# Hybrid mLSTM / neighbourhood / memory encoder layer on one Trainium2 core: the first loads and the last product rearranged

## Chip, core and metric

The kernel runs on one core of one Trainium2 (trn2) chip. The metric is the device time of one execution in microseconds (us). Engines: PE is TensorE (matmuls; PEld its weight loads), ACT is ScalarE, DVE is VectorE, POOL is GpSimd, SP is SyncE, which here issues every DMA.

## The reference, cut to what matters

One encoder layer over 2048 tokens of width 1024, all in float32. Three token mixers read one normalised input, are gated and merged, and go through `w_out` into the residual; a squared-ReLU MLP follows. At the two ends of the program, which the change touches, this is computed:

```
k, v = split(rmsnorm(mem, g_mem) @ w_mem_kv)     # 256 memory tokens: the first matmuls of the kernel
...
x = x + y @ w_out
u = rmsnorm(x, g_ffn) @ w_up
return x + square(relu(u)) @ w_down              # the last matmuls of the kernel, and the residual
```

## The kernel before, in words

**Arithmetic.** A float32 operand is split into a high part (`hi`, rounded to the PE's fp32r format by an ACT copy) and a low part (`lo = x - hi`, a DVE subtraction). `mm3` (L227 to L234) makes one product of three matmuls: hi*hi (L232), hi*lo (L233), lo*hi (L234). So the first of the three needs only the ACT copies, and the second needs the DVE's low part of the weights.

**Phases.** Phase 1 projects the input and runs the attention parts, phase 2 the mLSTM, phase 3 the merge, `w_out` and the MLP. The order of the PE's instructions is the program's own order (`manual_schedule`); on the other engines a scheduler orders the instructions when the program is built, by priority (program order, shifted by `cur_priority`) and readiness, and then each engine and each DMA queue works strictly in that order.

**Weights.** A weight unit is 128 x 1024 floats (512 KB). `fetch` (L156) takes the next unit of the plan: a DMA into a raw buffer (`wr`, a ring of WRAW = 3), then the ACT copy (L176) and the DVE subtraction (L177) into a split buffer (`ws`, a ring of WSP = 5). A raw buffer is free again when L177 has read it.

**The start** (`mem_setup`, L1085). SP issues `gmem`, then in turn two row blocks of `memT` (256 KB, L1094) and a unit of `w_mem_kv` (L172), four times. After the second pair come the first token tile `xt` and `gbc` (`prep_x`), whose square (L339), product (L341) and scaling (L342) stand among the splits on ACT and DVE. Each row block of `memT` is scaled and split into `hT` (ACT L1097, DVE L1098). Then PE runs the memory projection: for k = 0 to 7 two token tiles, three matmuls each, 48 matmuls of 128x512 in all; k = 0 and 1 use the first unit ("unit 0"), k = 2 and 3 unit 1, k = 4 and 5 unit 2, k = 6 and 7 unit 3. Jobs such as the transposes of the first token tile (L348) are slipped in between, and `block_a` follows.

**The end** (`mlp_down`, L1423). `w_down` is applied by a seven-product scheme (Strassen-Winograd) to a pair of token blocks. Each product runs over two slots of operands (`X`, split by L1461 and L1462), dq = 0 to 3, and within each dq over four token tiles t, each with a PSUM bank of its own: 4 x 4 x 3 = 48 matmuls. So all four banks are complete only in the last twelve matmuls. Then for each t DVE adds the bank to `acc` (L1488) and, where the output is final (`last`), forms `acc * r + x` with the residual `x` loaded from `x2` (L1495), and SP stores it (L101). The product that ends the kernel is number 6 (output 2).

Of the kernel before, what the change touches and what calls it, by code (L numbers as in the profile page):

```python
# [12 lines left out]
F32 = mybir.dt.float32  # L13
F32R = mybir.dt.float32r
BF16 = mybir.dt.bfloat16
AF = mybir.ActivationFunctionType
ALU = mybir.AluOpType
# [6 lines left out]
TB = 512  # L24
# [9 lines left out]
LATER_3 = 4  # L34
STORE = 'sync'
ORDER_0 = (2, 3, 0, 1)
WSP, WRAW, AHEAD = 5, 3, 5
NB = S // TB
SCRATCH = 1024
# [2 lines left out]
FF = 4096  # L42
# [38 lines left out]
class Body:  # L81
# [71 lines left out]
        up = [(u["up"][j][0], u["up"][j + 1][0], "sums") for j in range(0, FF // 128, 2)]  # L153
        return out + (u["proj"] + u["w_out"] + up) * (NB // 2)

    def fetch(self):  # L156

        nc = self.nc
        entry = self.wplan.pop(0)
        if len(entry) == 3:  # L160
            self.wready.append(self.fetch_sums(*entry[:2]))
            return
        i, nk = entry
        self.n += 1
        raw = self.p_w.tile([128, 1056], F32, name=f"wr_{self.n}", tag="wraw", bufs=WRAW)
        w = self.p_ws.tile([128, 2112], F32R, name=f"ws_{self.n}", tag="wsp", bufs=WSP)
        first = self.a["w_units"].shape[0]
        n = 1024 if i < first else 1056
        raw = raw[:, :n]

        w = w[:, :2 * n].rearrange("p (k l c) -> p l k c", k=nk, l=2)
        nc.sync.dma_start(raw, self.a["w_units"][i] if i < first else self.a["w_navm"][i - first])  # L172
        raw = raw.rearrange("p (k c) -> p k c", k=nk)
        prio = self.tc.cur_priority
        self.tc.cur_priority = prio + self.later
        nc.scalar.activation(w[:, 0], raw, AF.Copy)  # L176
        nc.vector.tensor_tensor(w[:, 1], raw, w[:, 0].bitcast(F32), ALU.subtract)  # L177
        self.tc.cur_priority -= self.later
        self.wready.append(w)
# [905 lines left out]
    def mem_setup(self):  # L1085
        nc, a, p_a = self.nc, self.a, self.p_a


        gm = p_a.tile([128, 8], F32, name="gmem")
        nc.sync.dma_start(gm, a["g_mem"])  # L1090
        mT = p_a.tile([128, 4 * 704], F32, name="memT", tag="nak", bufs=2)[:, :2 * D].rearrange("p (k t) -> p k t", k=8)
        later, self.later = self.later, 0
        for k in range(0, 8, 2):
            nc.sync.dma_start(mT[:, k:k + 2], a["memT"][k * 128:(k + 2) * 128].rearrange("(k p) t -> p k t", p=128))  # L1094
            for i in (k, k + 1):
                hi, lo, g = self.hT[:, 0, i, 0:256], self.hT[:, 1, i, 0:256], gm[:, i:i + 1]
                nc.scalar.activation(hi, mT[:, i], AF.Copy, scale=g)  # L1097
                nc.vector.scalar_tensor_tensor(lo, mT[:, i], g, hi.bitcast(F32), ALU.mult, ALU.subtract)  # L1098
            self.fetch()
            if k == 2:  # L1100
                self.prep_x(a["g_mix"])
        self.later = later
        w = self.take(4)
        self.prep_x()
        xs = p_a.tile([128, 4 * 704], F32, name="xstage", tag="nak", bufs=2)
        for i in range(2):
            self.prep_x(xt=xs[:, i * D:(i + 1) * D])
        gq = p_a.tile([128, 2], F32, name="gmqk_raw")
        nc.sync.dma_start(gq, a["g_mem_qk"])
        self.gmqk = p_a.tile([128, 2], F32, name="gmqk")  # L1110
        nc.vector.tensor_scalar(self.gmqk[:, 0:1], gq[:, 0:1], 0.125, None, ALU.mult)
        nc.vector.tensor_copy(self.gmqk[:, 1:2], gq[:, 1:2])
        self.mk = p_a.tile([128, 2, 2, 256], F32R, name="mk")
        self.mv = p_a.tile([128, 2, 256], F32, name="mv")
        ps = [self.ps("mx") for _ in range(2)]
        self.trans_x(MEM_T)
        for k in range(8):
            wk = w[k // 2]
            for t in range(2):
                self.mm3(ps[t], self.lhs_tok(self.hT, k, t), (wk[:, 0, k % 2], wk[:, 1, k % 2]), k == 0, k == 7)  # L1120
            self.tick()
        self.memz = []
        for t, p in enumerate(ps):
            z = self.t("zm", [128, 256], 4)
            nc.scalar.activation(z, p[:, 0:256], AF.Copy)
            nc.vector.tensor_copy(self.mv[:, t], p[:, 256:512])
            self.memz.append(z)
# [295 lines left out]
    def mlp_down(self, i, pair, then):  # L1423


        nc = self.nc
        S, T, B = (lambda n: ("s", n)), (lambda h, n: ("t", h, n)), (lambda h, n: ("b", h, n))

        products = ((("a", 0), B(0, 0), 0, False, 0), (("a", 1), B(0, 1), 1, False, 0), (S(1), T(1, 1), 0, True, 1),
                    (S(0), T(1, 0), 1, False, 3), (S(2), T(0, 0), 0, True, 3), (S(3), B(1, 1), 1, True, 1),  # L1430
                    (("a", 2), T(0, 1), 0, True, 2))
        acc = self.p_h.tile([128, 4, 4, 512], F32, name=f"acc{i}", tag="hT", bufs=1)
        todo = [(q + dq, p) for q in range(0, FF // 512, 2) for p in products for dq in range(2)]
        total, ready = len(todo), []
# [4 lines left out]
        ring = lambda n: [r for r in rings if r[0] <= n][-1]  # L1439

        def fetch():

            n = total - len(todo)
            q, (l, r, *_) = todo.pop(0)
            n0, _, places = ring(n)
            at = self.X[places[(n - n0) % len(places)]]
            raw = at[:, 1].bitcast(F32)
            raws = [raw[:, 0:2], raw[:, 2:4]]
            nc.sync.dma_start(raws[0], self.scr[l[0]][i][q][:, l[1]])
            if r[0] == "t":  # L1450
                nc.sync.dma_start(raws[1], self.scr["t"][q][:, r[1], r[2]])
            else:
                self.n += 1
                raws[1] = self.p_w.tile([128, 1056], F32, name=f"wr_{self.n}", tag="wraw", bufs=WRAW)[:, :1024].rearrange("p (u c) -> p u c", u=2)
                u = self.down[r[1] * FF // 256 + 2 * q][0]
                nc.sync.dma_start(raws[1], self.a["w_units"][u:u + 2, :, r[2] * 512:r[2] * 512 + 512].rearrange("u p c -> p u c"))
            prio = self.tc.cur_priority
            self.tc.cur_priority = prio + LATER_A
            for k, src in enumerate(raws):
                hi, lo = (at[:, h, 2 * k:2 * k + 2] for h in range(2))  # L1460
                nc.scalar.activation(hi, src, AF.Copy)  # L1461
                nc.vector.tensor_tensor(lo, src, hi.bitcast(F32), ALU.subtract)  # L1462
            self.tc.cur_priority -= LATER_A
            ready.append(at)
        sets = [[self.ps("mm") for _ in range(4)] for _ in range(2)]
        used, seen = 0, set()
        for q in range(0, FF // 256, 4):
            for _, _, s, more, out in products:
                for dq in range(4):
                    if dq % 2 == 0:  # L1470
                        while todo and len(ready) < ring(total - len(todo))[1]:
                            fetch()
                        if then and used in (32, 46):
                            self.load_mix(*then[used == 46])
                        used += 1
                        at = ready.pop(0)
                    d = dq % 2
                    for t, p in enumerate(sets[s]):
                        ts = slice(t * 128, t * 128 + 128)
                        self.mm3(p, (at[:, 0, d, ts], at[:, 1, d, ts]), (at[:, 0, 2 + d], at[:, 1, 2 + d]),  # L1480
                                 not more and dq == 0, dq == 3, more)
                last = q == FF // 256 - 4 and (out, s, more) in ((0, 1, False), (3, 0, True), (1, 1, True), (2, 0, True))
                for t, p in enumerate(sets[s]):
                    c = acc[:, out, t]
                    if out not in seen:
                        nc.scalar.activation(c, p, AF.Copy)
                    else:
                        nc.vector.tensor_tensor(c, c, p, ALU.add)  # L1488
                    if last:
                        j, half = out // 2, out % 2  # L1490
                        hs, r0 = slice(half * 512, half * 512 + 512), t * 128
                        x = self.ev()
                        nc.sync.dma_start(x, self.scr["x2"][pair[j]][r0:r0 + 128, hs])
                        n = 4 * pair[j] + t
                        nc.vector.scalar_tensor_tensor(x, c, self.r2[:, n:n + 1], x, ALU.mult, ALU.add)  # L1495
                        r0 += pair[j] * TB
                        self.store(self.a["out"][r0:r0 + 128, hs], x)
                seen.add(out)

            sets.reverse()  # L1500
# [75 lines left out]
```

## Time and profile before

| | us |
|---|---|
| three timed runs | 2989.27, 2983.28, 2989.30 (median 2989.27) |
| the profiled execution's own time | 2988.64 |
| its span (first to last instruction) | 2986.9 |
| PE busy | 2910.6 (97%) |
| DVE busy | 2070.4 (69%) |
| ACT busy | 1195.1 (40%) |
| mean granted PE clock | 0.995 of full speed |

The span is 1.74 us less than the execution's own time; the profile shows only the span. An engine's share is an average over three quite different phases. What an edit is worth has to be read at the place of the edit: what PE waits for there, what ends that wait, and where the next wait stands.

### The profile page before, as it was taken

What the parts mean: (1) busy time and instruction counts of PE and PEld (TensorE: products, weight loads), DVE (VectorE), ACT (ScalarE), POOL (GpSimd) and SP (SyncE); (2) the same over time, 40 slices, a digit from 0 to 9 for tenths busy, and PEclk for the clock granted to TensorE, in tenths of its full rate; (3) what the DMA queues carried; (4) which work ended last, traced back from release to release, by engine and by line L of the source; (5) the groups of instructions that cost most, each with busy time, mean ns of one, the idle gap of its engine ahead of it and who ended that gap; (6) DMA issues with size and microseconds to landing.
All of it is one profiled execution on the core that took longest, in us unless ns stands there. A gap on an engine that the chain in (4) does not pass through costs nothing.

```text
span 2986.9 us, 41900 instructions
## 1 busy us (share of the span) xinstructions
PE 2910.6 (97%) x15028; PEld 2374.8 (80%) x15028; DVE 2070.4 (69%) x3557; ACT 1195.1 (40%) x2198; POOL 237.1 (8%) x389
## 2 busy tenths in 40 slices
PE   8999999999999899999999999999999999999999
PEld 6778788878877677778888888888878888888887
DVE  6676775567654765674769888666676888885666
ACT  6454654344543333342233333543312433344331
POOL 3020210011000322330000000000000000000000
PEclk9999999999999999999999999999999999999999
DMA  8776777867799667789535444766874444466655
GB/s 276 225 253 202 231 227 240 266 217 217 240 283 307 195 199 234 240 276 315 183 110 169 155 152 155 275 191 224 268 235 128 137 155 151 154 226 225 195 182 165
DMA packets 341712, 632.97 MB, mean 212 GB/s; under 512 B 29344, under 2 KB 151008, under 8 KB 341504
## 3 DMA queue, kind: packets, MB, share of 16 engines
q1 hardware_dynamic: 341504, 630.30, 65.4%
q8 instruction: 118, 1.93, 0.3%
q14 instruction: 90, 0.74, 0.1%
HBM read 453.63 MB, written 176.55 MB: 211 GB/s over the span
## 4 chain that ended last, share of the span: by engine, by line
PE 55%; DVE 2%; DMA 2%; issue 1%; ACT 0%; POOL 0%; SPq 0%; DVEq 0%; ACTq 0%; POOLq 0%
PE mm L232 18%; PE mm L234 18%; PE mm L233 18%; PE mm L1339 0%; DVE h L900 0%; DMA og<-s_o 0%; DMA wr<-in_w_units_dram 0%; DMA hf<-s_hf 0%; DVE ev L1495 0%; ACT hf L896 0%; POOL rs L325 0%; DVE acc L1488 0%; DVE ws L177 0%; DVE h L888 0%; DMA X<-s_a 0%
## 5 line engine op out<-in xcount | busy, mean ns | idle before, releaser
L232 PE MATMUL mm<-X,ws 128*128 128x512 f32 x1152 | 448.5, 389 | 0.0
L234 PE MATMUL mm<-X,ws 128*128 128x512 f32 x1152 | 448.2, 389 | 0.0
L233 PE MATMUL mm<-X,ws 128*128 128x512 f32 x1152 | 448.1, 389 | 0.0
L232 PE MATMUL mm<-hT,ws 128*128 128x512 f32 x896 | 375.6, 419 | 12.1 <-ACT cz L654 5.5
L177 DVE TENSOR_TENSOR ws<-wr,ws 128x1024 fp32r<-128x1024 f32 (+1 forms) x212 | 263.0, 1246 | 142.8 <-ACT ws L176 137.7
L234 PE MATMUL mm<-hT,ws 128*128 128x512 f32 x896 | 353.6, 395 | 0.0
L233 PE MATMUL mm<-hT,ws 128*128 128x512 f32 x896 | 353.4, 394 | 0.0
L233 PE MATMUL mm<-X 128*128 128x512 f32 x896 | 348.8, 389 | 2.5 <-DVE X L1462 2.5
L234 PE MATMUL mm<-X 128*128 128x512 f32 x896 | 348.7, 389 | 0.5 <-DVE X L1462 0.5
L232 PE MATMUL mm<-X 128*128 128x512 f32 x896 | 348.7, 389 | 0.4 <-ACT X L1461 0.4
L1461 ACT ACTIVATE X<-X 128x1024 fp32r<-128x1024 f32 x176 | 187.0, 1063 | 319.4 <-DMA X<-s_t 124.5
L1462 DVE TENSOR_TENSOR X<-X 128x1024 fp32r<-128x1024 f32 x176 | 214.3, 1224 | 132.8 <-ACT X L1461 132.0
L176 ACT ACTIVATE ws<-wr 128x1024 fp32r<-128x1024 f32 (+1 forms) x212 | 223.5, 1059 | 164.7 <-PE mm L234 91.8
L232 PE MATMUL mm<-ws,hT 128*128 128x512 f32 (+2 forms) x704 | 260.9, 371 | 9.3 <-ACT cz L654 5.1
L234 PEld LDWEIGHTS mm<-X,ws 128*128 128x128 f32 x1152 | 216.2, 188 | 45.1
L233 PEld LDWEIGHTS mm<-X,ws 128*128 128x128 f32 x1152 | 216.2, 188 | 44.9
L232 PEld LDWEIGHTS mm<-X,ws 128*128 128x128 f32 x1152 | 216.2, 188 | 44.5
L234 PE MATMUL mm<-ws,hT 128*128 128x512 f32 (+2 forms) x704 | 249.8, 355 | 1.1 <-DVE hT L434 1.1
L233 PE MATMUL mm<-ws,hT 128*128 128x512 f32 (+2 forms) x704 | 249.0, 354 | 0.3 <-DVE ws L177 0.3
L202 ACT ACTIVATE ws<-wr 128x512 fp32r<-128x512 f32 x224 | 135.3, 630 | 219.9 <-PE mm L234 139.3
L232 PEld LDWEIGHTS mm<-hT,ws 128*128 128x128 f32 x896 | 170.2, 190 | 54.1 <-issue 9.8
L234 PEld LDWEIGHTS mm<-hT,ws 128*128 128x128 f32 x896 | 169.6, 189 | 39.0
(266 smaller groups left out, 4855.3 us busy)
## 6 DMA issues: line engine op xcount, KB each, us to landing
wr<-in_w_units_dram SPq DMA_DIRECT2D x308, 512.0 KB
s_s<-u SPq DMA_DIRECT2D x32, 1024.0 KB
X<-s_s SPq DMA_DIRECT2D x64, 512.0 KB
X<-s_t SPq DMA_DIRECT2D x64, 512.0 KB
s_g<-ev SPq DMA_DIRECT2D x96, 256.0 KB
ev<-s_g SPq DMA_DIRECT2D x96, 256.0 KB
s_a<-u SPq DMA_DIRECT2D x96, 256.0 KB
X<-s_a SPq DMA_DIRECT2D x48, 512.0 KB
```

Of the source, the lines that this page charges most:

```text
L176: nc.scalar.activation(w[:, 0], raw, AF.Copy)
L177: nc.vector.tensor_tensor(w[:, 1], raw, w[:, 0].bitcast(F32), ALU.subtract)
L202: nc.scalar.activation(hi, src, AF.Copy)
L232: mm(out, lhs[0], rhs[0], start=first, stop=False)
L233: mm(out, lhs[0], rhs[1], start=False, stop=False)
L234: mm(out, lhs[1], rhs[0], start=False, stop=last)
L1461: nc.scalar.activation(hi, src, AF.Copy)
L1462: nc.vector.tensor_tensor(lo, src, hi.bitcast(F32), ALU.subtract)
```

## The change

It has two parts, at the two ends of the program.

*At the start*, 11 matmuls of the 128x128 matrix `ones` with itself (plain f32) go to PE ahead of everything, into a PSUM tile that nobody reads. The first `memT` load is cut into its two row blocks, and the first weight unit is loaded and split in two halves of 128 x 512 (k = 0 and k = 1), each with its own ACT copy and DVE subtraction. SP's order becomes: memT block 0, unit 0 half 0, unit 0 half 1, memT block 1, then as before.

*At the end*, the last product of all runs token tile by token tile: t outside, dq inside, so that a bank is complete after each twelve matmuls. Ahead of it, both its slots are taken, the four residual tiles are loaded, and `acc * r` is added to each of them. After each tile's twelve matmuls one DVE instruction forms `psum * r + x`, and the tile is stored. The other products keep their order.

```diff
+WARM = 11
...
-    def fetch(self):
+    def fetch(self, halves=False):
...
-        nc.sync.dma_start(raw, self.a["w_units"][i] if i < first else self.a["w_navm"][i - first])
+        src = self.a["w_units"][i] if i < first else self.a["w_navm"][i - first]
+        if halves:
+            src, r = src.rearrange("p (k c) -> p k c", k=nk), raw.rearrange("p (k c) -> p k c", k=nk)
+            for k in range(nk):
+                nc.sync.dma_start(r[:, k], src[:, k])
+                nc.scalar.activation(w[:, 0, k], r[:, k], AF.Copy)
+                nc.vector.tensor_tensor(w[:, 1, k], r[:, k], w[:, 0, k].bitcast(F32), ALU.subtract)
+            self.wready.append(w)
+            return
+        nc.sync.dma_start(raw, src)
...
+        p = self.ps("mx")
+        for i in range(WARM):
+            nc.tensor.matmul(p[:, 0:128], self.ones, self.ones, start=True, stop=True)
...
         for k in range(0, 8, 2):
-            nc.sync.dma_start(mT[:, k:k + 2], a["memT"][k * 128:(k + 2) * 128].rearrange("(k p) t -> p k t", p=128))
+            load = lambda i, n: nc.sync.dma_start(mT[:, i:i + n], a["memT"][i * 128:(i + n) * 128].rearrange("(k p) t -> p k t", p=128))
+            if k == 0:
+                load(0, 1)
+                self.fetch(True)
+                load(1, 1)
+            else:
+                load(k, 2)
...
-            self.fetch()
+            if k:
+                self.fetch()
...
+        def part(p, at, t, dq, more):
+            d, ts = dq % 2, slice(t * 128, t * 128 + 128)
+            self.mm3(p, (at[:, 0, d, ts], at[:, 1, d, ts]), (at[:, 0, 2 + d], at[:, 1, 2 + d]),
+                     not more and dq == 0, dq == 3, more)
...
+        def finish(out, t, x, src):
+
+            r0, hs, r = place(out, t)
+            nc.vector.scalar_tensor_tensor(x, src, r, x, ALU.mult, ALU.add)
+            self.store(self.a["out"][r0:r0 + 128, hs], x)
...
+                if q == FF // 256 - 4 and n == 6:
+
+                    ats, xs = [slot(), slot()], [x2(out, t) for t in range(4)]
+                    for t in range(4):
+                        nc.vector.scalar_tensor_tensor(xs[t], acc[:, out, t], place(out, t)[2], xs[t], ALU.mult, ALU.add)
+                    for t, p in enumerate(sets[s]):
+                        for dq in range(4):
+                            part(p, ats[dq // 2], t, dq, more)
+                        finish(out, t, xs[t], p)
+                    break
```

`slot` is the old code that takes the next slot, `x2` the old load of the residual tile, `place` the old row and column arithmetic, each as a function.

## Rows read from the trace of the kernel before

**Rows 1.** Page, busy time and share of the span of the engines.

```profile
PE 2910.6 (97%) x15028; PEld 2374.8 (80%) x15028; DVE 2070.4 (69%) x3557; ACT 1195.1 (40%) x2198; POOL 237.1 (8%) x389
```

**Rows 2.** Timeline, end of the span: start, duration, engine, line, what, idle before.

```profile
2967.74 1.37 DVE L1488 TENSOR_TENSOR acc<-acc,mm 128x512 f32<-128x512 f32 x2 [5.67 <-PE mm L234]
...
2971.54 1.41 DVE L1495 SCALAR_TENSOR_TENSOR ev<-acc,r,ev 128x512 f32<-128x512 f32 x2
...
2978.62 1.37 DVE L1488 TENSOR_TENSOR acc<-acc,mm 128x512 f32<-128x512 f32 x2 [5.67 <-PE mm L234]
...
2980.23 0.39 PE L234 MATMUL mm<-X 128*128 128x512 f32 x1
...
2982.42 1.41 DVE L1495 SCALAR_TENSOR_TENSOR ev<-acc,r,ev 128x512 f32<-128x512 f32 x2
2983.20 0.99 SPq L101 DMA_DIRECT2D out_dram<-ev  x2
```

**Rows 3.** Timeline, SP's queue near the end: the last residual loads.

```profile
2962.52 3.35 SPq L1493 DMA_DIRECT2D ev<-s_x  x3
```

**Rows 4.** One line's instructions: a scalar_tensor_tensor that reads PSUM (ns min/median/max).

```profile
L1286 DVE SCALAR_TENSOR_TENSOR ev<-ev,mm x96: 679/686/690, 1402.7 to 2276.1; 128x512 f32<-128x512 f32 x96
```

**Rows 5.** Timeline, PE's first products.

```profile
7.50 0.80 PE L232 MATMUL mx<-ws,hT 128*128 128x512 f32 x1 [7.50 <-ACT ws L176]
8.76 0.80 PE L233 MATMUL mx<-ws,hT 128*128 128x512 f32 x1 [0.46 <-DVE ws L177]
...
12.34 0.63 PE L232 MATMUL mx<-ws,hT 128*128 128x512 f32 x1
...
12.76 0.46 PE L233 MATMUL mx<-ws,hT 128*128 128x512 f32 x1
...
15.83 0.39 PE L234 MATMUL mx<-ws,hT 128*128 128x512 f32 x1
...
16.05 0.39 PE L232 MATMUL mx<-ws,hT 128*128 128x512 f32 x1
...
16.73 0.50 PE L233 MATMUL mx<-ws,hT 128*128 128x512 f32 x1 [0.29 <-DVE ws L177]
```

**Rows 6.** Timeline, ACT and DVE at the start, up to unit 2's low part.

```profile
1.07 0.17 DVE L283 MEMSET ones<- 128x128 f32 x1
...
10.06 1.23 DVE L177 TENSOR_TENSOR ws<-wr,ws 128x1024 fp32r<-128x1024 f32 x1 [0.57 <-ACT ws L176]
...
12.25 0.91 ACT L1097 ACTIVATE hT<-memT,gmem 128x256 fp32r<-128x256 f32 x2 [0.89 <-DMA memT<-in_memT_dram]
...
13.32 1.15 ACT L342 ACTIVATE xt<-xt,rs 128x1024 f32<-128x1024 f32 x1 [0.16 <-POOL rs L325]
...
14.38 1.05 ACT L176 ACTIVATE ws<-wr 128x1024 fp32r<-128x1024 f32 x1
...
15.45 1.22 DVE L177 TENSOR_TENSOR ws<-wr,ws 128x1024 fp32r<-128x1024 f32 x1 [1.78 <-ACT ws L176]
```

**Rows 7.** Timeline, SP's first issues.

```profile
1.23 0.42 SPq L1094 DMA_DIRECT2D memT<-in_memT_dram  x1
1.70 0.46 SPq L172 DMA_DIRECT2D wr<-in_w_units_dram  x1
```

**Rows 8.** Busy time by stretch: PE, PEld, DVE, ACT, POOL, granted clock, DMA share, GB/s.

```profile
8.00:13.00 5.00, 4.54 (x11) 3.38 (x11) 4.09 (x6) 3.21 (x6) 1.47 (x2) 1.00 1.02 392
...
60.00:90.00 30.00, 26.25 (x147) 22.17 (x146) 24.39 (x49) 11.08 (x23) 7.30 (x4) 0.94 0.87 270
```

**Rows 9.** Timeline, a pair of f32 matmuls of 128 columns.

```profile
1054.46 0.38 PE L838 MATMUL mx<-ident,qk 128*128 128x128 f32 x2
```

**Rows 10.** Timeline, PE's next wait after the memory projection, and ACT ahead of it.

```profile
23.27 1.06 ACT L176 ACTIVATE ws<-wr 128x1024 fp32r<-128x1024 f32 x1 [0.51 <-DMA wr<-in_w_units_dram]
...
31.15 0.50 PE L234 MATMUL mm<-ws,hT 128*128 128x512 f32 x1 [1.10 <-DVE hT L434]
```

**Rows 11.** Timeline, PE after a longer wait, in the stretch from 60 to 90.

```profile
80.07 0.39 PE L232 MATMUL mm<-ws,hT 128*128 128x272 f32 x1 [2.37 <-ACT cz L654]
```

More of the change, by code (lines that the diff above doesn't have):

```diff
@@ L1466, in mlp_down, with slot @@
         used, seen = 0, set()
-        for q in range(0, FF // 256, 4):
-            for _, _, s, more, out in products:
-                for dq in range(4):
[L1470 to L1477, printed above, removed]
+        def slot():
+            nonlocal used
+            while todo and len(ready) < ring(total - len(todo))[1]:
+                fetch()
+            if then and used in (32, 46):
+                self.load_mix(*then[used == 46])
+            used += 1
+            return ready.pop(0)
@@ new lines, in part, with place, x2 @@
+        def part(p, at, t, dq, more):
+            d, ts = dq % 2, slice(t * 128, t * 128 + 128)
+            self.mm3(p, (at[:, 0, d, ts], at[:, 1, d, ts]), (at[:, 0, 2 + d], at[:, 1, 2 + d]),
+                     not more and dq == 0, dq == 3, more)
+        def place(out, t):
+            j, half, n = out // 2, out % 2, 4 * pair[out // 2] + t
+            return n * 128, slice(half * 512, half * 512 + 512), self.r2[:, n:n + 1]
+        def x2(out, t):
+            x = self.ev()
+            r0, hs, _ = place(out, t)
+            b = r0 // TB
+            nc.sync.dma_start(x, self.scr["x2"][b][r0 - b * TB:r0 - b * TB + 128, hs])
+            return x
@@ new lines, in finish @@
+        def finish(out, t, x, src):
+            r0, hs, r = place(out, t)
+            nc.vector.scalar_tensor_tensor(x, src, r, x, ALU.mult, ALU.add)
+            self.store(self.a["out"][r0:r0 + 128, hs], x)
+        for q in range(0, FF // 256, 4):
+            for n, (_, _, s, more, out) in enumerate(products):
+                if q == FF // 256 - 4 and n == 6:
[7 more added lines that the diff above has]
+                    break
+                for dq in range(4):
+                    at = at if dq % 2 else slot()
@@ L1478, in mlp_down @@
                     for t, p in enumerate(sets[s]):
[L1479 to L1482, printed above, removed]
+                        part(p, at, t, dq, more)
+                last = q == FF // 256 - 4 and (out, s, more) in ((0, 1, False), (3, 0, True), (1, 1, True))
@@ L1489, in mlp_down @@
                     if last:
[L1490 to L1497, printed above, removed]
+                        finish(out, t, x2(out, t), c)
                 seen.add(out)
```

## The prediction
> **What bounds the kernel now.** I read the busy shares first: PE is busy for 97% of the span [rows 1], so nothing but PE time, or time in which PE cannot run, is to be won. The 76 us of its idle time lie in many places; the change touches two, the first 17 us and the last 6. About 0.2% (6 us) is what a measurement of this kernel can tell from no change, so the question is whether these two places together hold that much.
>
> *The end.* The last matmul of the program starts at 2980.23 and ends at 2980.62. DVE then is in the middle of eight instructions that it began at 2978.62, when the first of the four banks was complete; the last residual is formed at 2983.83, and the last store is issued behind it [rows 2]. From there to the end of the span (2986.9) are 3.07 us of store and closing. So 3.21 us of DVE work lie bare behind PE.
>
> *The start.* PE's first product waits until 7.50, its second until 8.76, both for unit 0's split; between 8.76 and 12.76 nine products start in 4.00 us, 0.44 each, where from 15.83 to 16.05 the distance is 0.22 to 0.23 [rows 5]. That is the low and the high level of the clock (1.2 and 2.4 GHz); the granted-clock column reads 1.00 in that stretch [rows 8], so I go by the distance. Then comes the row that decides: at 16.73 PE waits again, for the low part of unit 2 [rows 5]. That part is formed by DVE from 15.45 to 16.67, from ACT's copy at 14.38, which stands in ACT's queue behind a scaling at 13.32 and two `memT` splits at 12.25; and those waited 0.89 us for their load [rows 6]. In that stretch the DMA share is 1.02 at 392 GB/s [rows 8]: the loads come as fast as they can. So PE's progress before 16.73 does not matter; the load stream sets that point.
>
> **The change part by part.**
>
> *Last product by token tile.* The 48 matmuls stay 48 with the same shapes; PE ends at 2980.62 as before. Bank 3 is complete only there, but banks 0 to 2 are complete 12, 24 and 36 matmuls earlier (12 x 0.227 = 2.72 us apart). Removed behind PE: what is left of four additions and four residual steps. Added behind PE: one scalar_tensor_tensor that reads PSUM, 0.69 us by the nearest row of that kind [rows 4]. DVE is done at 2980.66 + 0.69 = 2981.35 in place of 2983.83: **-2.48 us**. The four additions made beforehand (4 x 0.70 = 2.8 us, half a pair's 1.41) have the time from 2972.95, when DVE ends the product before [rows 2], to 2980.66, and only 2.1 us of earlier tiles' final steps beside them: they cost nothing, and without that cover 2.8 us. Their residual loads are the same four, issued by 2965.87 [rows 3], 4 us before the product starts; both operand slots were split long before. What is late next is the store itself: its 3.07 us stay. Bounds: one more DVE instruction before the last one leaves 1.7; if the last store, now without a neighbour issued 0.66 us ahead of it, also lands that much sooner, 3.1.
>
> *Halves of the first unit.* Half a copy, half a subtraction and half a load (256 KB at 392 GB/s) are 0.53 + 0.61 + 0.65 us less before the second product, and the second `memT` block (128 KB, 0.33 us) goes behind: about 2.1 us earlier, an estimate from those rows [rows 6, 8]. *Products of ones.* If the clock is high by then, nine products cost 2.0 us in place of 4.0 [rows 5]: 2.0 more. PE would be 4.1 us ahead. But then it has unit 1 to wait for (its low part ends at 11.29 [rows 6]), needs 11 x 0.227 us from there, is done at 13.8, and stands until unit 2's low part at 16.67. **All of it goes into that wait: 0 us.** Even with the clock low throughout the old kernel came to that point with no more than 0.7 us to spare, so neither edit can show behind it.
>
> Does unit 2 move? SP gets two more issues, 0.47 us each [rows 7]: everything behind is issued 0.94 us later, but with the DMA engines full (share 1.02) an issue is not what is late; without that cover, +0.94. The bytes and their order are the same. ACT and DVE get one instruction more each for unit 0, hidden in their waits before 12.25. If the scheduler put unit 2's copy ahead of the scaling at 13.32, unit 2 would come 1.06 us sooner. So the start lies between -1.06 and +0.94; I take 0, as the queues' order follows a program order that the change leaves alone there.
>
> **Sum**: 2988.64 - 2.48 + 0 = **2986.2 us** for the profiled execution, which lies 0.63 below the median of the three runs (2989.27).
>
> **The rivals.**
>
> *The start comes through.* If unit 2 is not the wall that I read (the scheduler orders the first 30 us anew, so that loads and splits keep up), the whole 4.1 us could reach the end: 2982.1. For it: the first 12 us of PE are plainly slow. Against: two further waits of the same kind, the one at 16.73 and one of 1.10 us at 31.15, the latter behind a DVE queue that starts from a load landing at 23.27 [rows 10].
>
> *A new gap brings the low clock back.* PE now stands from 13.8 to 16.7 with one product between. In the stretch 60 to 90 a wait of 2.37 us [rows 11] goes with a granted clock of 0.94 [rows 8]: 6% of 30 us, 1.8 us of PE time. Here that would strike the products after 16.7; the 1.10 us that PE waits at 31.15 [rows 10] take up most, 0.7 is left: 2986.9, and 2988.0 if none is taken up. The Trainium skill's page "TensorE: Matmul & The Clock Gate", section "Why this matters for your kernels", recommends a warm-up by matmuls and says that gaps between bursts bring the low clock back. By its first half the products of ones would be worth the 2.0 us of clock; the trace agrees on the slow first products, but the wait at 16.73 stands behind them. Its second half is this rival, and the stretch with 0.94 agrees with it.
>
> *The products of ones hold PE up* (slower). PE works in order, so the first real product waits for all 11. An f32 matmul appears as a pair of instructions: 0.38 us a pair at the high clock [rows 9], so at most 0.38 a piece at the low one. `ones` is written by 1.24 [rows 6]; 22 x 0.38 from 1.3 ends at 9.7, and the 24 products of units 0 and 1 (5.4 us at the high clock) still end at 15.1, before the wall. Above 0.44 us a piece they pass it. The other end is PE's first lone product, 0.80 [rows 5]: 17.6 + 5.4 us end at 24.3, 7.9 late, 6.8 after the slack at 31.15: 2993.0. It makes the kernel slower than before from 0.60 a piece on. Against: the pair has just this shape, and the 0.80 is a 512-column product.
>
> *The end does not shrink.* If the additions beforehand stand behind a late residual load, or the scheduler puts them last, the 2.48 is gone: 2988.6.
>
> **How the numbers follow.** Forecast 0.67; start comes through 0.14; low clock 0.09; end does not shrink 0.06; ones hold PE up 0.04. The forecast's own range is 2985.5 to 2987.9 by its bounds on the end and to about one us more either way by those on the start. The executions before lie between 2983.28 and 2989.30, which alone is 0.2%. Low end: the start comes through (2982.1), less 0.6 for the upper bound of the end: 2981.5. High end: the end does not shrink, with the 0.94 of the issues: 2989.6. Faster by over 0.2% means below 2983.3: the start coming through, and a little of the spread: 0.17. Slower by over 0.2%: above 2995.2: 0.04, the ones and some reordering. The rest, 0.79, is within 0.2%.
>
> **What would show it.** Right: PE's second product near 6.7 and at the high clock, but a longer wait at 16.7 for unit 2's low part, and from there the old times; at the end one DVE instruction of 0.7 us behind PE's last matmul, and the span 2.5 us shorter. Wrong: unit 2's low part ready well before 16.67, or PE's wait at 31.15 gone and everything after it earlier; slow products after 16.7; real products that wait for ones; or additions of `acc * r` behind PE's last matmul.

## The result, and the profile after

| | kernel before | changed kernel |
|---|---|---|
| median of 8 runs each | 2989.28 us | 2995.51 us |
| lowest and highest | 2980.35 and 2993.09 | 2991.38 and 2998.77 |
| the profiled execution's own time | 2988.64 | 2995.25 |
| its span | 2986.9 | 2993.5 |

The changed kernel is slower: ratio 1.0029, 95% interval 1.0019 to 1.0039, which is 8.7 us (the two medians are 6.2 us apart). The forecast was 2986.2 with a range from 2981.5 to 2989.6; the measured time lies above the range, on the side that had a chance of 0.04. The engines' busy times hardly differ [rows 1]; PE is busy for longer than before, with 22 instructions more:

```profile
PE 2919.1 (98%) x15050; PEld 2383.3 (80%) x15050; DVE 2070.2 (69%) x3558; ACT 1195.7 (40%) x2199; POOL 236.6 (8%) x389
```

To see where the time went I laid the two traces side by side and took, for each product, its start after less its start before. At 12.3 us PE is 4.0 us ahead; at 16.7 it is 1.2 behind, at 31 2.3 behind. Over the middle of the program this goes up and down by some microseconds: it is -0.8 at 2137 and +0.6 at 2175.6. Within one product it then jumps to +9.2, and it is still +9.0 at the last matmul. So three places have to be read: the two that the prediction looked at, and one at 2176 us that it did not.

**The end** came out as predicted. Timeline of the changed kernel, DVE, then PE's last matmul (start, duration, engine, line, what, idle before):

```profile
2982.71 0.74 DVE L1526 SCALAR_TENSOR_TENSOR ev<-acc,r,ev 128x512 f32<-128x512 f32 x1
...
2986.93 0.75 DVE L1518 SCALAR_TENSOR_TENSOR ev<-mm,r,ev 128x512 f32<-128x512 f32 x1 [1.97 <-PE mm L244]
2989.65 0.75 DVE L1518 SCALAR_TENSOR_TENSOR ev<-mm,r,ev 128x512 f32<-128x512 f32 x1 [1.97 <-PE mm L244]
...
2989.23 0.39 PE L244 MATMUL mm<-X 128*128 128x512 f32 x1
```

The fourth early addition (L1526) is over long before the last bank is complete. One DVE instruction stands behind PE's last matmul; DVE is done 0.78 us after PE (2990.40 - 2989.62), where it was 3.21 us [rows 2], and 3.1 us of store and closing follow as before.

**The start.** Timeline of the changed kernel, PE up to 34 us:

```profile
1.28 5.06 PE L1104 MATMUL mx<-ones 128*128 128x128 f32 x22 [1.28 <-DVE halo L402]
5.99 0.61 PE L242 MATMUL mx<-ws,hT 128*128 128x512 f32 x1
...
8.75 0.39 PE L244 MATMUL mx<-ws,hT 128*128 128x512 f32 x1
11.23 0.50 PE L242 MATMUL mx<-ws,hT 128*128 128x512 f32 x1 [2.10 <-ACT ws L186]
12.49 0.50 PE L243 MATMUL mx<-ws,hT 128*128 128x512 f32 x1 [0.76 <-DVE ws L187]
...
13.44 0.63 PE L243 MATMUL mx<-ws,hT 128*128 128x512 f32 x1
13.87 0.63 PE L244 MATMUL mx<-ws,hT 128*128 128x512 f32 x1
...
17.89 0.50 PE L243 MATMUL mx<-ws,hT 128*128 128x512 f32 x1 [0.76 <-DVE ws L187]
...
33.48 0.72 PE L244 MATMUL mm<-ws,hT 128*128 128x512 f32 x1 [2.26 <-DVE hT L444]
```

The first twelve real products now run from 5.99 to 8.75, 0.25 us each: the high clock almost from the start, and 4 us earlier. But PE then waits for unit 1, the clock falls (0.43 between the starts at 13.44 and 13.87; the granted clock of 13 to 17 us is 0.57), and the wait for unit 2's low part ends at 17.89, where it was 16.73 [rows 5]. DVE, then ACT, of the same stretch:

```profile
11.22 1.23 DVE L187 TENSOR_TENSOR ws<-wr,ws 128x1024 fp32r<-128x1024 f32 x1 [1.45 <-ACT ws L186]
...
16.62 1.23 DVE L187 TENSOR_TENSOR ws<-wr,ws 128x1024 fp32r<-128x1024 f32 x1 [1.75 <-ACT ws L186]
...
13.45 0.91 ACT L1117 ACTIVATE hT<-memT,gmem 128x256 fp32r<-128x256 f32 x2 [0.86 <-DMA memT<-in_memT_dram]
```

Units 1 and 2 are split 1.16 and 1.17 us later than before, and the `memT` load ahead of unit 2 comes 1.20 later [rows 6]. The DMA engines are as busy as before, but move less. Busy time from 4 to 8 us (PE, PEld, DVE, ACT, POOL, granted clock, DMA share, GB/s), the changed kernel and then the kernel before:

```profile
4.00:8.00 4.00, 4.00 (x19) 3.69 (x19) 2.26 (x4) 1.76 (x4) 0.00 (x0) 1.00 0.94 297
```

```profile
4.00:8.00 4.00, 0.50 (x1) 0.29 (x1) 1.40 (x3) 2.52 (x5) 0.00 (x0) 1.00 0.92 332
```

**The first call of `mlp_down`.** This is where the jump is. Timeline of the changed kernel, PE, around the seventh product of the first pair of token blocks (the first row is its first matmul, the last row the first matmul behind it):

```profile
2176.14 0.50 PE L242 MATMUL mm<-X 128*128 128x512 f32 x1 [0.15 <-ACT X L1482]
...
2178.64 0.50 PE L242 MATMUL mm<-X 128*128 128x512 f32 x1
2186.77 0.79 PE L243 MATMUL mm<-X 128*128 128x512 f32 x1 [7.62 <-DVE X L1483]
...
2190.34 0.61 PE L242 MATMUL mm<-X 128*128 128x512 f32 x1
2190.77 0.42 PE L243 MATMUL mm<-X 128*128 128x512 f32 x1
...
2198.09 0.39 PE L242 MATMUL mm<-X,ws 128*128 128x512 f32 x1
```

The same product of the kernel before:

```profile
2175.55 0.50 PE L232 MATMUL mm<-X 128*128 128x512 f32 x1 [0.35 <-ACT X L1461]
...
2181.94 0.39 PE L232 MATMUL mm<-X 128*128 128x512 f32 x1
2183.53 0.50 PE L233 MATMUL mm<-X 128*128 128x512 f32 x1 [1.20 <-DVE X L1462]
...
2188.87 0.39 PE L232 MATMUL mm<-X,ws 128*128 128x512 f32 x1
```

From its first matmul to the next product's: 13.32 us before, 21.95 after. The branch of the change asks for `q` and `n`, not for the call, and `mlp_down` is called twice. So the section on the change is wrong where it says that the last product of all has the new order and the others keep theirs: the seventh product of the first call has it too. In the second call all operands are there. In the first one the ring of operand slots is two deep for its last slots (`rings`, the entry with 2), since `load_mix` for the merge takes the other buffers, and a slot is split just when it is needed. In the old order PE needs the second slot after 24 matmuls; token tile by token tile it needs it after 6. And its splits stand in DVE's queue behind the early additions. The loads are not what is late: ACT's copy for this slot is done at 2178.59, while DVE works without a break until 2186.71. DVE of the changed kernel, then of the kernel before:

```profile
2181.05 0.74 DVE L1526 SCALAR_TENSOR_TENSOR ev<-acc,r,ev 128x512 f32<-128x512 f32 x1
2181.71 0.74 DVE L1518 SCALAR_TENSOR_TENSOR ev<-acc,r,ev 128x512 f32<-128x512 f32 x1
2182.37 2.07 DVE L1526 SCALAR_TENSOR_TENSOR ev<-acc,r,ev 128x512 f32<-128x512 f32 x3
2184.36 2.35 DVE L1483 TENSOR_TENSOR X<-X 128x1024 fp32r<-128x1024 f32 x2
```

```profile
2180.45 1.23 DVE L1462 TENSOR_TENSOR X<-X 128x1024 fp32r<-128x1024 f32 x1
...
2182.25 1.22 DVE L1462 TENSOR_TENSOR X<-X 128x1024 fp32r<-128x1024 f32 x1
```

The longer wait is 6.4 us of the 8.6. The rest is the clock: behind the gap the products start 0.43 us apart until 2190.77, at the low level, and 0.23 after. Busy time by stretch (columns as above), the changed kernel and then the kernel before:

```profile
8.00:13.00 5.00, 2.15 (x8) 1.23 (x8) 2.31 (x4) 3.12 (x5) 0.25 (x2) 1.00 1.01 371
...
2160.00:2190.00 30.00, 21.65 (x86) 16.63 (x85) 21.57 (x28) 6.07 (x6) 0.00 (x0) 0.84 0.80 278
```

```profile
2160.00:2190.00 30.00, 27.92 (x121) 22.14 (x120) 22.07 (x29) 6.25 (x6) 0.00 (x0) 1.00 0.83 281
```

PE's waits over the whole span, that for the low part of `X` alone (us in total, times, longest), after and before:

```profile
PE mm L243 <- DVE X L1483: 10.2, 2, 7.6
```

```profile
PE mm L233 <- DVE X L1462: 2.5, 2, 1.3
```

### The profile page after: what moved, and what is told of

Same layout as the page of the kernel before. It is cut to its first block, busy times and chain, and to the rows that moved or that the text cites. A ratio compares the mean times of both kernels' runs of the same rounds, so it can differ in the third digit from the quotient of the medians.

```text
span 2993.5 us, 41949 instructions
## 1 busy us (share of the span) xinstructions
PE 2919.1 (98%) x15050; PEld 2383.3 (80%) x15050; DVE 2070.2 (69%) x3558; ACT 1195.7 (40%) x2199; POOL 236.6 (8%) x389
## 4 chain that ended last, share of the span: by engine, by line
PE 58%; DVE 2%; DMA 1%; ACT 1%; issue 1%; POOL 0%; SPq 0%; DVEq 0%; ACTq 0%; POOLq 0%
PE mm L242 19%; PE mm L243 19%; PE mm L244 19%; PE pn L872 1%; PE mm L1360 0%; DMA hf<-s_hf 0%; DMA wr<-in_w_units_dram 0%; PE pn L875 0%; DVE h L910 0%; PE mx L881 0%; ACT hf L906 0%; POOL rs L335 0%; DVE ev L1518 0%; DMA X<-s_a 0%; DVE acc L1542 0%
## 5 line engine op out<-in xcount | busy, mean ns | idle before, releaser
L242 PE MATMUL mm<-hT,ws 128*128 128x512 f32 x896 | 376.4, 420 | 10.5 <-ACT cz L664 5.5
L242 PEld LDWEIGHTS mm<-hT,ws 128*128 128x128 f32 x896 | 170.5, 190 | 52.7 <-issue 8.3
L243 PEld LDWEIGHTS mm<-X 128*128 128x128 f32 x896 | 169.1, 189 | 46.1 <-DVE X L1483 10.9
```

The costliest lines, as they stand in the source:

```text
L242: mm(out, lhs[0], rhs[0], start=first, stop=False)
L243: mm(out, lhs[0], rhs[1], start=False, stop=False)
```

## The experiments

A ratio is to the kernel before, run beside the experiment on the same chip, with its 95% interval (the medians of the kernel before: 2986.45 us beside experiments 1 to 4, 2985.22 beside 5 to 8, 2986.51 beside 9 to 12, 2985.52 beside 13 to 15). The edits are given against the changed kernel or against an earlier experiment.

**1. The whole start, the end in the last call only.**

```diff
-                if q == FF // 256 - 4 and n == 6:
+                if q == FF // 256 - 4 and n == 6 and not then:
...
-                last = q == FF // 256 - 4 and (out, s, more) in ((0, 1, False), (3, 0, True), (1, 1, True))
+                last = q == FF // 256 - 4 and (out, s, more) in ((0, 1, False), (3, 0, True), (1, 1, True), (2, 0, True))
```

> The changed kernel with one condition more: the last product goes token tile by token tile only in the second call of mlp_down (the one that ends the kernel); the first call keeps the old order. Theory A: the loss sits in the first call, where the product's second operand slot is needed after 12 matmuls and not after 24, and waits 7.62 us in the changed kernel (9.0 us with the clock that falls). Then the loss is gone and the gain at the end stays: 2989.3 - 2.4 = 2986.9, between 2984 and 2989, and no wait of several us near 2180. Rival B: the later loads of the start (shift +3.9 us at 33 us) carry through, and the wait near 2187 is only where that lands: then it stays at 2992 or more. Rival C: the scheduler's new order in phases 1 and 2 is the cause: also above 2990.

Median 2990.48, ratio 1.0012 [1.0001, 1.0023]. The wait in the first call is 1.21 us again and the product takes 13.32. So the loss in the first call is gone, as theory A has it; the time is above theory A's range all the same, and what the whole start has to do with that is taken up in 9 to 15. (The expectation says that the slot is needed after 12 matmuls; by the edit and the trace it is after 6.)

**2. The start alone**: the kernel before with the halves, the new order of loads and the 11 products of ones.

> The kernel before with the start of the change alone (products of ones, halves). Theory A: no loss and no gain that lasts, 2989.3 with 2 us either way; unit 2's low part comes about 1.2 us later than in the kernel before, as in the changed kernel, and later waits take that up. Rival B: 2993 to 2996. If the start is worth its 4 us after all: 2985.

Median 2988.55, ratio 1.0004 [0.9995, 1.0012]: theory A, within the runs' spread.

**3. The end in both calls, with the old start**: the kernel before with the new `mlp_down`.

> The kernel before with the last product's new order in both calls and the old start. Theory A: a wait of 6 to 8 us in the first call's last product, the low clock behind it, and 2.4 us less at the end: 2989.3 + 9 - 2.4 = 2996, between 2993 and 2998. Rival B: the wait is that of the kernel before (1.2 us), and the time 2987.

Median 2992.08, ratio 1.0018 [1.0007, 1.0030]. The time lies 0.9 us below theory A's range; PE's timeline has the long wait that it foresaw, without anything of the start:

```profile
2182.49 0.79 PE L233 MATMUL mm<-X 128*128 128x512 f32 x1 [7.51 <-DVE X L1462]
```

**4. The end in the last call only, with the old start**: experiment 3 with the edit of experiment 1.

> The kernel before with the new order in the last call alone, old start. All theories: the end is 2.4 us shorter (one DVE instruction of 0.75 us behind PE's last matmul), all else as in the kernel before: 2986.9. Nothing is moved ahead of the last call, so the order of the queues before it is the old one; if the time differs by more than 1 us from this, the runs' own spread is that large.

Median 2984.16, ratio 0.9992 [0.9982, 1.0003]. Timeline of the end, DVE and PE:

```profile
2980.67 0.75 DVE L1497 SCALAR_TENSOR_TENSOR ev<-mm,r,ev 128x512 f32<-128x512 f32 x1 [1.97 <-PE mm L234]
...
2980.24 0.39 PE L234 MATMUL mm<-X 128*128 128x512 f32 x1
```

This execution's last matmul happens to start at the very time of the kernel before (2980.23 [rows 2]); its span is 2984.4 in place of 2986.9. From the start of the last matmul to the end of the span it is 4.16 us in place of 6.67, and 4.16 again in experiment 11, where that matmul starts at 2973.64. So the end alone is worth 2.5 us, as predicted, and experiments 3 and 4, which differ in the first call alone, are 0.26% (7.9 us) apart.

**5. Only the order of the matmuls in the first call** (experiment 4, and there the tile order without early additions).

```diff
+                if q == FF // 256 - 4 and n == 6:
+
+                    ats = [slot(), slot()]
+                    for t, p in enumerate(sets[s]):
+                        for dq in range(4):
+                            part(p, ats[dq // 2], t, dq, more)
+                        c = acc[:, out, t]
+                        nc.vector.tensor_tensor(c, c, p, ALU.add)
+                        finish(out, t, x2(out, t), c)
+                    break
```

> The kernel with the new end in the last call alone and the old start (2984.2 before), plus this in the first call: its last product goes token tile by token tile, but the residual is not added beforehand; each tile is added to acc and finished as in the kernel before. So DVE's queue ahead of the second slot's splits is the old one, and only the need for that slot comes earlier. Theory A1, both halves share the loss: the slot's first low part is done at about 2183.5 as in the kernel before, PE asks for it at 2178.9; the wait is about 4.5 us, of which 2.7 are lost (12 products that could be done meanwhile are not), and up to 2 us of low clock: 2987 to 2989. Theory A2, the early additions alone make the loss: 2984. Theory A3, the order of the tiles alone makes it: 2992, wait 7 us.

**6. Only the early additions in the first call** (experiment 4, and there the old order with the additions ahead).

```diff
+                if q == FF // 256 - 4 and n == 6:
+
+                    ats, xs = [slot(), slot()], [x2(out, t) for t in range(4)]
+                    for t in range(4):
+                        nc.vector.scalar_tensor_tensor(xs[t], acc[:, out, t], place(out, t)[2], xs[t], ALU.mult, ALU.add)
+                    for dq in range(4):
+                        for t, p in enumerate(sets[s]):
+                            part(p, ats[dq // 2], t, dq, more)
+                    for t, p in enumerate(sets[s]):
+                        finish(out, t, xs[t], p)
+                    break
```

> The same base; in the first call the four residual tiles are loaded and added beforehand, as in the changed kernel, but the product runs in the old order (second slot after 24 products). Theory A1: the four additions of 0.75 us stand ahead of the second slot's two low parts in DVE's queue, which end at about 2186.7 in place of 2183.5; PE asks at 2182.2, waits 4.4 us in place of 1.2: 2987 to 2989.5. Theory A2: 2992. Theory A3: 2984.

Medians 2989.04 (ratio 1.0015 [1.0004, 1.0026]) and 2986.43 (1.0003 [0.9993, 1.0013]). Against experiment 4, their base (0.9992, on another chip), that is +0.23% and +0.11%. Runs alone would not part experiment 6 from the kernel before; the traces do. PE of experiment 5, then of experiment 6 with its DVE:

```profile
2172.55 0.50 PE L232 MATMUL mm<-X 128*128 128x512 f32 x1 [0.39 <-ACT X L1461]
...
2180.53 0.79 PE L233 MATMUL mm<-X 128*128 128x512 f32 x1 [4.95 <-DVE X L1462]
...
2192.05 0.39 PE L232 MATMUL mm<-X,ws 128*128 128x512 f32 x1
```

```profile
2167.58 0.41 PE L232 MATMUL mm<-X 128*128 128x512 f32 x1
...
2178.11 0.50 PE L233 MATMUL mm<-X 128*128 128x512 f32 x1 [3.81 <-DVE X L1462]
...
2180.09 0.63 PE L234 MATMUL mm<-X 128*128 128x512 f32 x1
...
2185.10 0.39 PE L232 MATMUL mm<-X,ws 128*128 128x512 f32 x1
...
2173.72 2.07 DVE L1515 SCALAR_TENSOR_TENSOR ev<-acc,r,ev 128x512 f32<-128x512 f32 x3
2175.70 2.35 DVE L1462 TENSOR_TENSOR X<-X 128x1024 fp32r<-128x1024 f32 x2
```

The table takes the seventh product of the first call from its first matmul to the first behind it, as above.

| first call | PE's wait for the slot's low part | the product takes |
|---|---|---|
| as before (kernel before) | 1.20 us | 13.32 us |
| early additions alone (6) | 3.81 | 17.52 |
| tile order alone (5) | 4.95 | 19.50 |
| both (3; changed kernel; the same again, 9) | 7.51; 7.62; 7.60 | 22.24; 21.95; 22.89 |

Each half costs by itself, the order 6.2 us and the additions 4.2; together it is 8.6 to 9.6. This is theory A1. The two halves can be told apart in DVE's queue: the low part that PE waits for is done 7.9 us after the product's first matmul in the kernel before and in experiment 5, 10.6 and 10.5 in the changed kernel and experiment 6. So the additions make the slot later, and the order makes PE ask sooner. The added waits sum up (3.75 + 2.61 = 6.36, against 6.31 to 6.42 with both); the low clock behind the wait comes in each case, but with both only once: in experiment 6 some eight products start 0.43 us apart instead of 0.23, 1.6 us.

**7 and 8. The parts of the start, with the end in the last call only**: experiment 4 with the 11 products of ones alone, and experiment 4 with the halves and the new order of loads alone.

> New end in the last call alone, plus the eleven products of ones at the start; loads whole as in the kernel before. If my reading of the start holds: the first products of PE run at the high clock, unit 2's low part stands where it stood (begins 15.3 to 15.6), the time is that without the ones, 2984.2, within 1.5 us. If the ones hold PE or bring a low clock in a later gap: 2986 or more. If the start's clock is worth something after all: 2982.

> New end in the last call alone, plus the halves of the first unit, without the ones. Unit 2's low part begins 1.2 us later than in the kernel before (16.6 in place of 15.45), since the loads behind come later by the two issues more; the wait of PE at 31 us grows as in the changed kernel. If the start's cost of some 3 us is that of the halves: 2987 to 2988. If it is that of the ones: 2984.2.

Medians 2983.19 (0.9989 [0.9979, 0.9999]) and 2984.43 (0.9991 [0.9983, 1.0000]). Neither part costs anything here. But neither has the early high clock, which experiment 7 was expected to have: there PE waits 1.37 us between the ones and the first real product, and the products from 9.00 to 11.56 start 0.43 us apart (in experiment 8 those from 6.63 to 9.19). Busy time by stretch of experiment 7, with a granted clock of 0.66:

```profile
8.00:13.00 5.00, 4.55 (x13) 3.62 (x14) 4.35 (x7) 3.37 (x6) 1.76 (x2) 0.66 1.05 407
```

In experiment 8 unit 2 is late as in the changed kernel, without a single product of ones:

```profile
16.99 1.23 DVE L187 TENSOR_TENSOR ws<-wr,ws 128x1024 fp32r<-128x1024 f32 x1 [1.71 <-ACT ws L186]
```

**9 to 12. The changed kernel and experiments 1, 4 and 7 again, on another chip.**

> The changed kernel as it is, once more, beside the three below on one chip. The parts so far: order of the first call's last product +8 (both calls 2992.1, last call alone 2984.2), end -2.3, start between 0 and +4. So 2986 + 8 - 2.4 = 2992 with a start that costs nothing, 2995 with one that costs 3.

> The whole start with the new end in the last call alone, once more: it stood at 2990.5, where its parts one by one (ones 2983.2, halves 2984.4, end 2984.2) would give 2984. If the start as a whole costs nothing, the first figure was spread of the runs: 2983 to 2986 now. If ones and halves together cost what neither does alone: 2988 or more.

> New end in the last call alone, old start, once more: 2.4 us below the kernel before, 2983 to 2985.

> New end in the last call alone plus the ones, once more. By my reading the ones are worth nothing behind unit 2's wait: the time of the run without them, within 1.5 us. If they are worth 1 us or more it stands below that run a second time.

Changed kernel: 2995.12 in 5 runs, 1.0035 [1.0021, 1.0049]. Experiment 1 again: 2987.93, 1.0011 [1.0000, 1.0021]. Experiment 4 again: 2983.77, 0.9994 [0.9985, 1.0003]. Experiment 7 again: 2988.10, 1.0006 [0.9995, 1.0016]. So the first call costs what it did (9 less 10: 0.24%), and the whole start costs again (10 less 11: 0.17%; 1 less 4: 0.20%), though experiment 10 lands between its two cases and settles neither. The ones alone give 0.9989 (experiment 7) and 1.0006 (experiment 12), where experiment 4 has 0.9992 and 0.9994: no effect that the runs agree on, and the second is well above the 1.5 us that were expected at most.

**13 to 15. What it is in the start**: experiment 1 with 4 products of ones in place of 11; experiment 1 with the first `memT` load whole again (one issue more than before, where the change has two); experiment 8 again.

```diff
-WARM = 11
+WARM = 4
```

> The whole start and the new end in the last call alone, but 4 products of ones in place of 11, so that PE is idle again well before the first real product. Theory S1 (the ones bring the high clock early, it falls in the waits behind and falls more often later: mean granted clock 0.9925 with ones, 0.9935 without): 2984 to 2985.5, mean clock 0.9935. Theory S2 (the ones cost by being there: a PSUM buffer taken, other instruction places): 2988 to 2989, as with 11. Theory S3 (later loads): 2988 too.

```diff
-                load(0, 1)
+                load(0, 2)
                 self.fetch(True)
-                load(1, 1)
```

> The whole start and the new end in the last call alone, but the first two memT blocks in one load ahead of unit 0's halves: one SP issue less, and PE's first product some 0.3 us later. S3: unit 2's low part 0.5 us sooner and half the cost gone: 2986 to 2987. S1 and S2: 2988 to 2989, no change.

> Halves and the new end in the last call, no ones, once more. S1 and S2: 2984.4 again. S3: the first figure was low by chance, and 2987 to 2988 comes now.

Medians 2984.59 (0.9998 [0.9989, 1.0007]), 2985.09 (1.0002 [0.9993, 1.0011]) and 2984.43 (0.9996 [0.9987, 1.0005]): the three intervals overlap, and all of them include no change. None of the theories fits all three: S1 foresaw the time of experiment 13, but not its clock (0.9930 in place of 0.9935) and not that experiment 14 comes down with all 11 ones; S2 wanted 2988 to 2989 in 13 and 14; S3 wanted 2988 in 13 and 2987 to 2988 in 15. DVE's row for unit 2 in experiments 13 and 14:

```profile
16.44 1.23 DVE L187 TENSOR_TENSOR ws<-wr,ws 128x1024 fp32r<-128x1024 f32 x1 [1.75 <-ACT ws L186]
```

```profile
16.01 1.23 DVE L187 TENSOR_TENSOR ws<-wr,ws 128x1024 fp32r<-128x1024 f32 x1 [1.79 <-ACT ws L186]
```

Over all traces: with the old loads this split starts between 14.75 and 15.58 (8 traces), with two issues more between 15.92 and 16.99 (8 traces), with one more at 16.01. The two groups do not overlap; the one trace with one issue more lies near the lower edge of the second. The DMA rate from 4 to 8 us parts the same traces: 332 to 386 GB/s with the old loads, 258 to 312 with the first unit in halves (experiment 14: 310).

## Why the prediction was wrong, point by point

**The step that failed is the first one, "Last product by token tile".** It costed the edit once, at the end of the program, and said that "both operand slots were split long before". That holds for the second call of `mlp_down`; the code stands in a function that runs twice, and in the first call the second slot is split just in time. What the runs showed in its place is a loss of 8.6 us there by the trace, +0.26% and +0.24% by the runs (experiments 3 less 4, 9 less 10), and both halves of the edit have a share in it (experiments 5 and 6). Two views of the trace before would have shown it. One line's instructions, of the line that the change replaces, count 32 from 2130.2 to 2983.1, sixteen for each call:

```profile
L1495 DVE SCALAR_TENSOR_TENSOR ev<-acc,r,ev x32: 746/748/758, 2130.2 to 2983.1; 128x512 f32<-128x512 f32 x32
```

And PE's wait of 1.20 us at 2183.53, shown above, says that this slot has no slack: whoever needs it 18 matmuls (4.1 us) sooner waits that much longer, and 2.8 us of DVE work put ahead of it come on top. From those two rows and the prediction's own 2.8 us, 1.2 + 4.1 + 2.8 = 8.1 us of wait would have been the estimate, and 5.3 for the order alone and 4.0 for the additions alone; the runs showed 7.62, 4.95 and 3.81 (changed kernel, experiments 5 and 6).

**The size of the end** was right: -2.48 predicted, -2.5 by the span of experiment 4, -0.08% and -0.06% by the runs of experiments 4 and 11 (both intervals still touch 1). That residual loads would be no hindrance was right too, and the rival in which the end does not shrink fell.

**The start's wall** was right as a mechanism and wrong in one term. PE's gain of 4 us did go into the wait for unit 2, as said. But the 0 that I took for the loads behind does not hold: they are split 1.2 us later, a little beyond the bound of +0.94. The prediction had "the bytes and their order are the same" and took the rate as the same too. At much the same DMA share the engines moved 297 GB/s in place of 332 from 4 to 8 us, and 371 in place of 392 from 8 to 13 [rows 8]. How much of the 1.2 us comes from this lower rate and how much from the two issues is not shown: no run has more issues with whole loads. That an issue is not what is late while the engines are full is therefore neither shown nor refuted. PE leaves its wait at 31 us 2.3 us later than in the trace before [rows 10].

**What the whole start costs in the end is smaller and not settled.** The pairs 1 less 4 and 10 less 11 put it at 0.20% and 0.17%, 4 to 6 us; experiment 2 less the kernel before at 0.04%. Later loads alone do not explain it, since experiments 8 and 15 have them and lose nothing. For the ones alone 7 and 12 go apart. With 4 ones, or with one issue less, it is 0.05% and 0.09% above the end alone (0.9998 and 1.0002, against 0.9992 and 0.9994), too little for the runs to tell from none. Taken together, the five kernels with 11 ones and the new end in the last call only (1, 7, 10, 12, 14) have a mean ratio of 1.0004, the four without ones (4, 8, 11, 15) 0.9993; and their mean granted clocks are 0.9925 to 0.9931, against 0.9933 to 0.9941. So 11 ones may cost some 0.1%, with the halves or without; one by one their ratios range from 0.9989 to 1.0012, and where the time would go was not found.

**The rivals.** That the ones hold PE up fell by the first row of PE: 22 instructions from 1.28 to 6.34 are 0.23 us each, far from the 0.60 at which they would decide, and the first real product starts at 5.99 in place of 7.50. They do hold it a little: it starts without a wait right behind them, where without ones it starts at 5.31 and 5.24 (experiments 8 and 15), and the wall covers that. That the start comes through fell with unit 2. That a new gap brings the low clock back is what happened, but mostly elsewhere: at 13 to 16 us it cost nothing, since the wall at 17.89 stood behind it, and at 2187, where the prediction had no gap, it took some 2 us. The Trainium skill's page "TensorE: Matmul & The Clock Gate", section "Why this matters for your kernels", which the prediction weighed, warns of gaps between bursts; the granted clock of 0.84 in 2160 to 2190, against 1.00 before, agrees with it.

**The sum by the runs**: end -0.07%, first call +0.25%, start +0.17 to +0.20%, together +0.35 to +0.38%; measured 0.29% and 0.35%. With experiment 2's 0.04% for the start the sum would be 0.22%; the runs fix the start's share no better than that. The version that takes the good part alone is experiment 4: 0.9992 and 0.9994, 2.3 and 2.7 us below the kernel before by medians, and 2.5 by the trace.

## What to carry to other kernels

Before costing an edit, count how often its line runs and where: the same product of the same function has slack in one call and none in another, because the buffers around it differ. Bringing one bank's end forward means needing its last operand sooner, and work done "beforehand" stands in a queue ahead of something; a short wait of the kernel before at that operand is the warning. And speeding up the first products was worth nothing here, as the load behind them sets the pace.

## What the runs showed of the hardware that was not expected

A nearly full share of the DMA engines was not one rate: from 4 to 8 us they moved 332 GB/s at a share of 0.92 with the old loads, and 297 at 0.94 with the first unit and the first `memT` load cut in halves; the loads behind were usable 1.2 us later.

A plain f32 product of 128x128 appears as two instructions, of 0.23 us each here from the first of the program on; I had allowed for 0.38.

In the changed kernel waits of 2.10 and 0.76 us ended at 11.23 and 12.49, and the products from 13.44 on ran at the low level. Behind the 3.81 us of experiment 6 the low level came 1.3 us into the next products; behind the 7.62 us of the changed kernel the next products were at it at once.

Runs of one and the same kernel spread over some 10 us (the kernel before: 2979.57 to 2990.40 in the 27 runs beside experiments 9 to 12), so that an effect of 2 or 3 us has to be read in the trace at its place, and one that has no place, like what the start costs in the end, stays open.
